# A scan's unused operand read from a PSUM bank, and new instruction lengths in the order planner

## The chip, the cores and the metric

The kernel runs on one core of one Trainium2 chip. The metric is the device time of one execution in microseconds (us); three executions of the kernel before took 1605.84, 1606.33 and 1608.09 us, median 1606.33 us. A profiled execution of it spans 1604.8 us from its first to its last instruction.

## What is computed

One layer of a hybrid block on 2048 tokens of width 1024, in fp32:

```python
hn = rmsnorm(h, mix_norm_g)
u, g_ssm, q, k, v, g_attn = split(hn @ w_in)                 # six times 512 columns
y_ssm = glu(gelu(s5_scan(u))) * silu(g_ssm)                  # diagonal complex SSM, 32 groups
y_att = stick_breaking(rmsnorm(q), rmsnorm(k), v) * silu(g_attn)   # 8 heads of 64
h = h + concat(y_ssm, y_att) @ w_out
h = h + sigmoid(rmsnorm(h) @ w_pg) * (p @ w_pp)
```

The change sits in the attention. For a block of 128 queries, with `z = q k^T / 8`:

```python
log_stay = where(s < t, log_sigmoid(-z), 0)
later    = reverse_cumsum(log_stay) - log_stay               # over the keys after s
weights  = where(s < t, exp(log_sigmoid(z) + later), 0)
out      = weights @ v
```

The kernel computes the same with products: `sigmoid(-z)` is multiplied up from the last key to the first, and each `sigmoid(z)` is multiplied with the running product of the keys behind it.

## The kernel before

**Stages.** The program falls into three stretches of the span. Up to about 345 us it normalizes and turns x, projects u (`phase_u`), prepares and runs the S5 scan (`ssm_chain`, `ssm_pack`, `ssm_batch`) and the SSM gate (`gate_unit`). From 345 us to about 1180 us it runs the attention, four pairs of heads (`hp`) whose 16 query blocks are swept with a skew of 8 steps, mixed with the projections of the blocks to come (`attn_proj`, matmuls L657 to L659 into `ps_qk`) and, in its last quarter, with the GLU (`glu_unit`, matmuls L542 to L544 into `ps_g` and `ps_v`). From there to the end it runs the output projection and the per-layer embedding (`out_block`, `ple_block`), which are TensorE work almost alone.

**One attention step** (`attn_block`) handles one chunk of up to 512 keys for two heads `h`. On TensorE (PE) six matmuls, L718, fill two PSUM tiles `z`, one for each head. For each head ScalarE (ACT) writes `px = sigmoid(-z)`, L723, and `be = sigmoid(z)`, L728. On the chunk of the diagonal GpSimd (POOL) masks both, L732. VectorE (DVE) runs the product through `px` in place, from the last key to the first, L734; its first element is the one the next chunk goes on from (`carry`, copied by L727). POOL multiplies `be` with the shifted `px`, L736. PE turns `be` into two PSUM tiles `ps_wt`, 16 transposes for a full chunk, L527 in `transposes`; ACT (L745) or DVE (L743) copies them to `ws`; PE multiplies with v into `ps_o`, L753. So what follows a chunk's `z` goes round PE, ACT, (POOL,) DVE, POOL, PE, ACT, PE.

**The scan.** L734 is a `tensor_tensor_scan` with `op0=mult` and `op1=bypass`: the state is multiplied with the first operand, and the second is read but not used. Before the change both operands are `px`, which lies in SBUF.

**PSUM.** There are eight banks with names. The `z` tiles go round three of them, "z0", "z1" and "tr", and round "z0" and "z1" alone in the last eight of the 40 steps (`BANKS`, `glu_at`). A bank is written again when all readers of its last tile are done.

**The order** of all instructions on every engine, and of the DMAs on their queues, is made before the run by a planner. `plan` collects each instruction's dependences from the memory it touches, and a length from `duration`: a pair of the time that the engine is taken and of a delay until the result can be used. `list_schedule` then goes through the program as if it ran, always giving the engine that is free first the instruction with the lowest rank that is ready; on PE a change between full matmuls, matmuls over 64 rows and matmuls over 64 columns costs `change=0.2`, and work of the present kind is preferred by `near=4.0`. `best_order` repeats this forwards and backwards six times and keeps the shortest plan; `arrange` fixes that order on each engine. Reads of a PSUM tile count as writes in `plan`, so a bank's readers stand one behind the other in the order of the program. The lengths are thus not times of the run, but they decide what stands where in all five queues.

Of the kernel before, what the change touches and what calls it, by code (L numbers as in the profile page):

```python
# [13 lines left out]
ALU = mybir.AluOpType  # L14
# [686 lines left out]
def attn_block(e, pool, A, i):  # L701
# [3 lines left out]
    nc = e.nc  # L705
    q, g = A.q.pop(i)
    half = [slice(HD * h, HD * (h + 1)) for h in range(HPP)]
    carry = [None] * HPP
    po = e.bank("ps_o", *e.o_banks)
    held = []  # L710
    for ch in range(i // 4, -1, -1):
        nb = min(4, i + 1 - 4 * ch)
        n = nb * P
# [6 lines left out]
        for h, z in enumerate(zs):  # L720
            be = e.buf("be", [P, 512], BEB, BEX)
            px = e.buf("px", [P, 513], PXB, PXX)
            nc.scalar.activation(px[:, :n], z[:, :n], AF.Sigmoid, scale=-(HD ** -0.5))  # L723
            if carry[h] is None:
                nc.gpsimd.memset(px[:, n:n + 1], 1.0)
            else:
                nc.vector.tensor_copy(px[:, n:n + 1], carry[h])  # L727
            nc.scalar.activation(be[:, :n], z[:, :n], AF.Sigmoid, scale=HD ** -0.5)  # L728
            if ch == i // 4:
                for a, fill in ((px, 1.0), (be, 0.0)):  # L730
                    d = a[:, n - P:n]
                    nc.gpsimd.affine_select(d, d, pattern=[[-1, P]], compare_op=ALU.is_gt, fill=fill, base=0, channel_multiplier=1)  # L732
            rv = px[:, :n][:, ::-1]
            nc.vector.tensor_tensor_scan(rv, rv, rv, initial=1.0 if carry[h] is None else carry[h], op0=ALU.mult, op1=ALU.bypass)  # L734
            carry[h] = px[:, 0:1]
            nc.gpsimd.tensor_tensor(be[:, :n], be[:, :n], px[:, 1:n + 1], op=ALU.mult)  # L736
            bes.append(be)
        w = e.buf("ws", [P, HPP, 4, P], WSB, WSX)
# [310 lines left out]
def duration(i, name, outs, ins, psum):  # L1049

    n = max([a[1] for a in outs + ins] or [1])
    eng = str(i.engine).split(".")[-1]
    if name == "InstDMACopy":
        return (0.6 if eng == "Pool" else 0.45), 0.0
    if name == "InstMatmult":
        cols, kind = outs[0][1], ins[0][2]
        if i.is_transpose:
            return (0.031 if ins[0][0] <= 64 else 0.109), 0.12
        if "float32r" in kind or "bfloat16" in kind:
            return {512: 0.228, 256: 0.120}.get(cols, max(cols / 2255.0, 0.058)) / (2 if ins[0][0] <= 64 else 1), 0.12  # L1060
        half = min(outs[0][0], ins[0][0]) <= 64
        return (1 if half else 2) * max(cols / 1160.0, 0.056), 0.12
    if eng == "Activation":
        return 0.193 + n * 0.00082, 0.0
    if eng == "Pool":
        if name == "InstTensorTensor" and "pow" in str(i.op).lower():
            return 0.45 + 0.15 * n, 0.0
        base, slope = {"InstMemset": (0.1, 0.0008), "InstTensorCopy": (0.5, 0.001), "InstTensorScalarPtr": (0.3, 0.001), "InstTensorScalarAffineSelect": (0.35, 0.0008)}.get(name, (0.47, 0.00175))
        return base + slope * n, 0.0
    if name == "InstTensorScalarPtr" and i.is_tensor_tensor_scan:  # L1070
        return 0.22 + n * 0.0027, 0.0
    if name in ("InstMemset", "InstTensorCopy") and not psum:
        return 0.11 + n * 0.0006, 0.0
    return 0.15 + n * 0.00107, 0.0


def plan(tc, pools):
# [3 lines left out]
    open_l, open_r, base, slots, spans, over, home, used = [], [], {}, {}, [], {}, {}, {}  # L1081
# [23 lines left out]
    for k, i in enumerate(mybir_i):  # L1105
        if type(i).__name__ == "BassTilePoolBoundary":
            pre.append(set())
            soft.append({number[q] for q in over.get(i.name, [])} | used.get(i.name, set()))
            length.append((0.0, 0.0, 0))
            continue  # L1110
        need, ins, outs, loose, psum = set(), [], [], set(), False
        for w, accs in ((0, i.ins), (1, i.outs)):
            for a in accs:
                b = getattr(a, "bass_ap", None)
# [4 lines left out]
                for s, c in a.ap[1:]:  # L1119
                    n *= int(c)  # L1120
                (outs if w else ins).append((int(a.ap[0][1]), n, str(a.dtype)))
                if type(t).__name__ != "Tile":
                    continue
                shape = tuple(int(x) for x in t.shape)
# [44 lines left out]
        loose.discard(k)  # L1169
        pre.append(need)  # L1170
        soft.append(loose - need)
        length.append(duration(i, type(i).__name__, outs, ins, psum) + ((outs[0][0] * outs[0][1] * 4 if type(i).__name__ == "InstDMACopy" else 0),))
        if type(i).__name__ == "InstMatmult":
            mode[k] = "rows" if ins[0][0] <= 64 else "cols" if outs[0][0] <= 64 else "all"
    return mybir_i, pre, soft, length, mode


_seen = {}
# [9 lines left out]
def list_schedule(ops, pre, soft, length, mode, rank, near=4.0, change=0.2):  # L1188
# [4 lines left out]
    after, open_, free, wait, ready, order, now = [[] for _ in ops], [len(p) + len(q) for p, q in zip(pre, soft)], {}, {}, {}, {}, {}  # L1193
    start, done, link = [0.0] * n, [0.0] * n, 0.0
    for k in range(n):
        for q in (*pre[k], *soft[k]):
# [16 lines left out]
    for _ in range(n):  # L1213
# [115 lines left out]
```

## Time and profile before

| what | value |
|---|---|
| median of three runs | 1606.33 us |
| span of the profiled execution | 1604.8 us |
| first `ps_z` matmul of the attention | 345.0 us |
| last `ps_z` matmul | 1171.2 us |
| DVE busy, 350 to 1200 us | 682.6 of 850 us |
| POOL busy, 350 to 1200 us | 634.6 of 850 us |
| ACT busy, 350 to 1200 us | 561.1 of 850 us |

The profile lists, for groups of instructions, a busy time and a mean duration; for stretches of the span, the busy time of each engine and the clock that TensorE was granted (1.00 is full); and a chain of waits, which goes back from the last instruction, at each step to what released it. Matmuls are pipelined, so the duration of one in the groups is longer than the time from one to the next; the pieces of the chain give that time.

### The profile page before, as it was taken

The numbers are of one execution on the slowest core, as the hardware profiler recorded it, in microseconds if no ns is written. First come the engines' busy times: TensorE is split into PE (matmuls) and PEld (weight loads), VectorE is DVE, ScalarE is ACT, GpSimd is POOL, SyncE is SP. The second block draws the span as 40 slices with busy tenths as digits, with TensorE's granted clock in tenths as the row PEclk, the third lists the DMA queues.
The fourth block names the chain that finished last, engine by engine and source line by source line (L and its number), as shares of the span: only waits on it lengthen the run. The fifth ranks groups of instructions, "written<-read, shape, count | busy, mean of one in ns | idle before, by whom it ended". The sixth has DMA issues, their size and how long they took to land.

```text
span 1604.8 us, 31108 instructions
## 1 busy us (share of the span) xinstructions
PE 1548.5 (96%) x11878; PEld 1254.5 (78%) x11878; DVE 1079.1 (67%) x1980; ACT 825.2 (51%) x1850; POOL 766.3 (48%) x882
## 2 busy tenths in 40 slices
PE   6999898999999999999999999999989999999998
PEld 6998888987777777777777776777678788888887
DVE  6895948868678997789987899748764432332322
ACT  6643435456566776677766777646544221121211
POOL 2242434437578898688967798747630000000000
PEclk9999999999999999999999999999999999999999
DMA  9897535455332323323233234432354221212210
GB/s 294 262 289 194 175 118 181 156 174 193 113 113 84 112 91 132 113 85 108 95 132 112 86 109 112 109 96 68 107 164 126 83 79 50 86 60 69 64 49 33
DMA packets 147670, 195.58 MB, mean 122 GB/s; under 512 B 63697, under 2 KB 110753, under 8 KB 136129
## 3 DMA queue, kind: packets, MB, share of 16 engines
q1 hardware_dynamic: 145552, 186.45, 36.1%
q0 software_dynamic: 1968, 7.15, 2.2%
q8 instruction: 94, 1.54, 0.4%
q14 instruction: 56, 0.45, 0.1%
HBM read 145.44 MB, written 48.12 MB: 121 GB/s over the span
## 4 chain that ended last, share of the span: by engine, by line
PE 79%; DVE 11%; issue 4%; POOL 3%; ACT 1%; DMA 1%; SPq 0%; POOLq 0%; DVEq 0%; ACTq 0%
PE ps_qk L657 7%; PE ps_qk L659 7%; PE ps_qk L658 7%; PE ps_o L753 6%; PE ps_z L718 5%; PE ps_wt L527 4%; PE ps_g L659 4%; PE ps_h L657 4%; PE ps_h L658 4%; PE ps_g L658 4%; PE ps_h L659 4%; PE ps_g L657 4%; DVE px L734 3%; POOL be L736 2%; PE ps_u L543 2%
## 5 line engine op out<-in xcount | busy, mean ns | idle before, releaser
L736 POOL TENSOR_TENSOR be<-be,px 128x512 f32<-128x512 f32 (+3 forms) x320 | 404.1, 1275 | 136.6 <-DVE px L734 51.0
L734 DVE TENSOR_TENSOR_SCAN px<-px 128x512 f32<-128x512 f32 (+3 forms) x320 | 424.6, 1338 | 52.6 <-ACT px L723 37.0
L723 ACT ACTIVATE px<-ps_z 128x512 f32<-128x512 f32 (+3 forms) x320 | 170.0, 539 | 78.8 <-PE ps_z L718 51.9
L657 PE MATMUL ps_qk<-w_w,xt 128*128 128x512 f32 x480 | 198.7, 414 | 1.2 <-DVE gn L60 1.2
L658 PE MATMUL ps_qk<-w_w,xt 128*128 128x512 f32 x480 | 195.4, 407 | 0.0
L659 PE MATMUL ps_qk<-w_w,xt 128*128 128x512 f32 x480 | 195.3, 407 | 0.0
L508 POOL TENSOR_TENSOR rs_h<-rs_h,mhalf 128x1 f32<-128x1 f32 x16 | 9.1, 572 | 381.8 <-DVE rs_h L67 381.8
L728 ACT ACTIVATE be<-ps_z 128x512 f32<-128x512 f32 (+3 forms) x320 | 170.4, 545 | 5.4 <-PE ps_wt L527 5.4
L745 ACT ACTIVATE ws<-ps_wt 128x512 f32<-128x512 f32 (+3 forms) x256 | 129.0, 540 | 79.3 <-PE ps_wt L527 78.5
L718 PE MATMUL ps_z<-k,q 64*128 64x512 f32 (+3 forms) x960 | 138.5, 392 | 2.4 <-ACT be L728 1.5
L753 PE MATMUL ps_o<-ws,v 128*64 128x128 f32 x2176 | 138.3, 278 | 0.0
L753 PEld LDWEIGHTS ps_o<-ws,v 128*64 128x64 f32 x2176 | 118.7, 138 | 22.2 <-issue 18.1
L527 PEld LDWEIGHTS ps_wt<-ident,be 64*128 64x128 f32 x2176 | 83.1, 138 | 51.6 <-issue 25.6
L657 PEld LDWEIGHTS ps_qk<-w_w,xt 128*128 128x128 f32 x480 | 90.2, 188 | 32.1 <-issue 11.9
L659 PEld LDWEIGHTS ps_qk<-w_w,xt 128*128 128x128 f32 x480 | 90.3, 188 | 24.2 <-issue 5.7
L658 PEld LDWEIGHTS ps_qk<-w_w,xt 128*128 128x128 f32 x480 | 90.5, 189 | 23.5 <-issue 5.8
L527 PE MATMUL ps_wt<-ident,be 64*128 64x64 f32 x2176 | 102.9, 229 | 5.8 <-POOL be L736 2.8
L514 ACT ACTIVATE yr<-yt 128x512 fp32r<-128x512 f32 x32 | 20.2, 632 | 162.7 <-PE ps_h L659 157.3
L657 PE MATMUL ps_h<-w_w,yr 128*128 128x512 f32 x256 | 100.7, 393 | 2.3 <-ACT yr L514 2.3
L659 PE MATMUL ps_g<-w_wg,hr 128*128 128x512 f32 x256 | 101.5, 397 | 0.0
L658 PE MATMUL ps_g<-w_wg,hr 128*128 128x512 f32 x256 | 101.1, 395 | 0.0
L658 PE MATMUL ps_h<-w_w,yr 128*128 128x512 f32 x256 | 100.6, 393 | 0.0
(378 smaller groups left out, 3608.5 us busy)
## 6 DMA issues: line engine op xcount, KB each, us to landing
xt<-hn SPq DMA_DIRECT2D x60, 1024.0 KB, 4.9
hn<-xt SPq DMA_DIRECT2D x16, 1024.0 KB, 9.5
wst<-in_w_in_dram SPq DMA_DIRECT2D x48, 256.0 KB, 5.3
xg<-hn SPq DMA_DIRECT2D x12, 1024.0 KB, 7.0
x<-in_x_dram SPq DMA_DIRECT2D x16, 512.0 KB, 7.0
out_dram<-o SPq DMA_DIRECT2D x32, 256.0 KB, 2.0
h<-in_x_dram SPq DMA_DIRECT2D x15, 512.0 KB, 4.3
u<-uq POOLq DMA_DIRECT2D x4, 1024.0 KB, 18.3
```

The source lines that it names most:

```text
L527: e.nc.tensor.transpose(ps[h][:, 64 * k:64 * k + 64], v[r], e.ident[r, r])
L543: mm(out, wh, xl, start=False, stop=False)
L657: mm(out, xh, wh, start=first, stop=False)
L658: mm(out, xh, wl, start=False, stop=False)
L659: mm(out, xl, wh, start=False, stop=last)
L718: nc.tensor.matmul(z[:, :n], q[half[h], a], A.k[ch][half[h], b, :n], start=s == 0, stop=s == 2)
L723: nc.scalar.activation(px[:, :n], z[:, :n], AF.Sigmoid, scale=-(HD ** -0.5))
L728: nc.scalar.activation(be[:, :n], z[:, :n], AF.Sigmoid, scale=HD ** -0.5)
L734: nc.vector.tensor_tensor_scan(rv, rv, rv, initial=1.0 if carry[h] is None else carry[h], op0=ALU.mult, op1=ALU.bypass)
L736: nc.gpsimd.tensor_tensor(be[:, :n], be[:, :n], px[:, 1:n + 1], op=ALU.mult)
L745: nc.scalar.activation(dst, ps, AF.Copy)
L753: nc.tensor.matmul(po[half[h], :P], A.v[sb][:, h], w[:, h, b], start=sb == i, stop=sb == 0)
```

## The change

The scan reads `z`, where it lies in PSUM, as its second operand. As before, the operand's values are not used. The planner gets other lengths for most instructions, and a resource that it did not have: an instruction that `shares` marks (a GpSimd instruction that reads SBUF, a DVE instruction with two operands in SBUF, or a DVE copy or scalar instruction from SBUF to SBUF) does not start before the last one so marked has ended.

```diff
-            nc.vector.tensor_tensor_scan(rv, rv, rv, initial=1.0 if carry[h] is None else carry[h], op0=ALU.mult, op1=ALU.bypass)
+            nc.vector.tensor_tensor_scan(rv, rv, z[:, :n][:, ::-1], initial=1.0 if carry[h] is None else carry[h], op0=ALU.mult, op1=ALU.bypass)
...
         if i.is_transpose:
-            return (0.031 if ins[0][0] <= 64 else 0.109), 0.12
+            return (0.031 if ins[0][0] <= 64 else 0.109), 0.11
         if "float32r" in kind or "bfloat16" in kind:
-            return {512: 0.228, 256: 0.120}.get(cols, max(cols / 2255.0, 0.058)) / (2 if ins[0][0] <= 64 else 1), 0.12
+            return max(cols / 2400.0 + 0.0136, 0.107) / (2 if ins[0][0] <= 64 else 1), 0.11
...
     if eng == "Activation":
-        return 0.193 + n * 0.00082, 0.0
+        return (0.05 if psum else 0.094) + n * 0.00083, 0.065 if psum else 0.03
     if eng == "Pool":
         if name == "InstTensorTensor" and "pow" in str(i.op).lower():
-            return 0.45 + 0.15 * n, 0.0
-        base, slope = {"InstMemset": (0.1, 0.0008), "InstTensorCopy": (0.5, 0.001), "InstTensorScalarPtr": (0.3, 0.001), "InstTensorScalarAffineSelect": (0.35, 0.0008)}.get(name, (0.47, 0.00175))
-        return base + slope * n, 0.0
+            return 0.35 + 0.15 * n, 0.08
+        base, slope = {"InstMemset": (0.04, 0.0008), "InstTensorCopy": (0.4, 0.001), "InstTensorScalarPtr": (0.25, 0.001), "InstTensorScalarAffineSelect": (0.14, 0.0008)}.get(name, (0.12, 0.00186))
+        return base + slope * n, 0.09
     if name == "InstTensorScalarPtr" and i.is_tensor_tensor_scan:
-        return 0.22 + n * 0.0027, 0.0
-    if name in ("InstMemset", "InstTensorCopy") and not psum:
-        return 0.11 + n * 0.0006, 0.0
-    return 0.15 + n * 0.00107, 0.0
+        return 0.05 + n * 0.0022, 0.03
+    if name in ("InstMemset", "InstTensorCopy", "InstTensorScalarPtr") and not psum and not i_tt(i):
+        return 0.07 + n * 0.0006, 0.03
+    return 0.07 + n * 0.00104, 0.03
...
+def shares(i, name, read, psum):
+
+    eng = str(i.engine).split(".")[-1]
+    if eng == "Pool":
+        return read > 0 and name != "InstDMACopy"
+    return eng == "DVE" and (read > 1 or (read == 1 and not psum and name in ("InstTensorCopy", "InstTensorScalarPtr")))
...
+        if length[k][3]:
+            t = max(t, port)
+            port = t + length[k][0]
```

No instruction is added or removed; all five queues are put in another order. On PE the attention gets other neighbours around the `z` tiles. The rows of PE around the pair of tiles `ps_z_6375` and `ps_z_6376` (one chunk of one query block, two heads; `ps_qk` is a projection, `ps_o` the product with v), before:

```order
L718 MATMUL ps_z_6375<-k_5136,q_5966 128x512
L718 MATMUL ps_z_6376<-k_5136,q_5966 128x512 [waits Activation_49]
L718 MATMUL ps_z_6375<-k_5136,q_5966 128x512
L718 MATMUL ps_z_6376<-k_5136,q_5966 128x512
L718 MATMUL ps_z_6375<-k_5136,q_5966 128x512
L718 MATMUL ps_z_6376<-k_5136,q_5966 128x512
L657 MATMUL ps_qk_6302<-w_w_4966,xt_6300 128x512
L658 MATMUL ps_qk_6302<-w_w_4966,xt_6300 128x512
```

and with the change:

```order
L718 MATMUL ps_z_6375<-k_5136,q_5966 128x512
L718 MATMUL ps_z_6376<-k_5136,q_5966 128x512 [waits DVE_49]
L718 MATMUL ps_z_6375<-k_5136,q_5966 128x512
L718 MATMUL ps_z_6376<-k_5136,q_5966 128x512
L718 MATMUL ps_z_6375<-k_5136,q_5966 128x512
L718 MATMUL ps_z_6376<-k_5136,q_5966 128x512
L753 MATMUL ps_o_6030<-ws_6061,v_5642 64x128 x2
L753 MATMUL ps_o_6030<-ws_6061,v_5344 64x128 x2
```

The bank is now waited for on DVE (its last reader is the scan) where it was on ACT, and behind the tiles stands other work.

On ACT the two sigmoids of the two heads `ps_z_10187` and `ps_z_10188` (another chunk) stood apart, before:

```order
L723 ACTIVATE px_10196<-ps_z_10187 128x512 [waits DVE_49,Pool_49]
L728 ACTIVATE be_10195<-ps_z_10187 128x512
L492 ACTIVATE w_w_10500<-wst_10501,gmix_121 128x512 [waits DMAHW2_49]
L694 ACTIVATE k_9268<-ps_tq_10025,gqk_2008 128x128 [waits DVE_49]
L723 ACTIVATE px_10203<-ps_z_10188 128x512 [waits Activation_49,Pool_49]
L514 ACTIVATE q_10077<-ps_tq_10078 128x128 [waits PE_49]
L728 ACTIVATE be_10202<-ps_z_10188 128x512
```

and stand together with the change:

```order
L723 ACTIVATE px_10196<-ps_z_10187 128x512 [waits PE_49,Activation_49,Pool_49]
L723 ACTIVATE px_10203<-ps_z_10188 128x512 [waits PE_49,DVE_49,Activation_49,Pool_49]
L728 ACTIVATE be_10195<-ps_z_10187 128x512
L697 ACTIVATE g_10086<-ps_tq_10078 128x128 [waits DVE_49]
L728 ACTIVATE be_10202<-ps_z_10188 128x512
```

On DVE the scans of the same two heads (the listing calls the scan SCALAR_TENSOR_TENSOR; `px_10196` and `px_10203`) had four instructions between them, before:

```order
L734 SCALAR_TENSOR_TENSOR px_10196<-px_10196,px_10141 128x512 [waits Activation_49]
L71 SCALAR_TENSOR_TENSOR k_9268<-ps_tq_10025,gqk_2008,k_9268 128x128 [waits Activation_49]
L60 TENSOR_TENSOR q_10077<-ps_tq_10078,q_10077 128x128 [waits Activation_49]
L60 TENSOR_TENSOR yat_9979<-ps_o_9886,g_9332 128x128 [waits DMAHW2_49]
L727 COPY px_10203<-px_10148 128x1 [waits DVE_49,Pool_49]
L734 SCALAR_TENSOR_TENSOR px_10203<-px_10203,px_10148 128x512
```

and follow each other with the change, each with its `z` tile as an operand:

```order
L727 COPY px_10196<-px_10141 128x1 [waits DVE_49]
L727 COPY px_10203<-px_10148 128x1 [waits DVE_49,Pool_49]
L71 SCALAR_TENSOR_TENSOR w_w_10515<-wst_10516,gmix_121,w_w_10515 128x512 [waits DMAHW7_49,Activation_49]
L734 SCALAR_TENSOR_TENSOR px_10196<-px_10196,px_10141,ps_z_10187 128x512 [waits Activation_49]
L734 SCALAR_TENSOR_TENSOR px_10203<-px_10203,px_10148,ps_z_10188 128x512 [waits Activation_49]
```

The two copies that start the scans moved ahead of both, and the small instructions between the scans elsewhere.

More of the change, by code (lines that the diff above doesn't have):

```diff
@@ L1121, in plan @@
                 (outs if w else ins).append((int(a.ap[0][1]), n, str(a.dtype)))
+                read += not w and n > 1 and type(t).__name__ == "Tile" and slots_space(slots, t.tag) == "SB"
                 if type(t).__name__ != "Tile":
```

12 lines of the change are left out of this document (8 added, 4 removed).

## The prediction

> **What bounds the kernel now.** I read the busy table first, then the stretches of the span, then the chain of waits, and last the groups that the change touches.
>
> ```profile
> PE 1548.5 (96%) x11878; PEld 1254.5 (78%) x11878; DVE 1079.1 (67%) x1980; ACT 825.2 (51%) x1850; POOL 766.3 (48%) x882
> PE 79%; DVE 11%; issue 4%; POOL 3%; ACT 1%; DMA 1%; SPq 0%; POOLq 0%; DVEq 0%; ACTq 0%
> 0.00:50.00 50.00, 34.22 (x318) 32.24 (x319) 34.96 (x140) 31.42 (x52) 15.53 (x26) 0.99 0.82 265
> 50.00:350.00 300.00, 281.14 (x2256) 271.80 (x2255) 225.44 (x479) 144.33 (x313) 107.06 (x71) 0.95 0.64 195
> 350.00:950.00 600.00, 597.42 (x5435) 445.94 (x5436) 495.14 (x885) 413.49 (x1034) 470.92 (x611) 1.00 0.33 113
> 950.00:1200.00 250.00, 237.43 (x1924) 181.21 (x1921) 187.43 (x261) 147.59 (x297) 163.66 (x160) 0.97 0.39 109
> 1200.00:1604.00 404.00, 398.26 (x1954) 323.25 (x1952) 136.11 (x219) 88.33 (x156) 9.14 (x16) 1.00 0.23 71
> ```
>
> The first row is the share of each engine; PE is busy for 96% of the span. The second is the chain of waits by engine: 79% of it is PE. The others are stretches; after each length stand the busy time of PE, weight loads, DVE, ACT and POOL, then PE's granted clock. PE lacks 15.8 us at the start (the first data), 18.9 us from 50 to 350, 2.6 us in the first 600 us of attention, 12.6 us in its last part, 5.7 us in the output stage. The last is not touched: no scan runs there, and POOL is busy 9 us of 404. So the attention, where the change works, can give back 15.2 us of idle PE, and 0.03 x 250 = 7.5 us where the clock was 0.97: **22.7 us, or 1.4%, is all that a perfect DVE and POOL could bring there**. The chain shows where it was lost, in stretches such as
>
> ```profile
> 976.11 1.14 POOL be L736
> 977.24 0.80 issue
> 978.04 1.20 POOL be L736
> ...
> 1091.60 1.19 DVE px L734
> ...
> 1174.81 6.51 DMA yt<-ys
> 1181.34 0.64 ACT yr L514
> ```
>
> (start, length, what): scans and multiplications end last there, 0.8 us lies between two multiplications, and the attention's last piece waits for a load that no scan is part of.
>
> **The scan's operand.** The groups, by form:
>
> ```profile
> L734 DVE TENSOR_TENSOR_SCAN px<-px 128x512 f32<-128x512 f32 x224 | 343.3, 1542 | 44.2 <-ACT px L723 37.0 <-POOL px L732 7.0
> L736 POOL TENSOR_TENSOR be<-be,px 128x512 f32<-128x512 f32 x224 | 322.1, 1450 | 117.0 <-DVE px L734 36.2 <-ACT be L728 29.4 <-DVE px L727 22.7
> L728 ACT ACTIVATE be<-ps_z 128x512 f32<-128x512 f32 x224 | 133.5, 610 | 4.2 <-PE ps_wt L527 4.2
> L723 ACT ACTIVATE px<-ps_z 128x512 f32<-128x512 f32 x224 | 133.2, 603 | 68.2 <-PE ps_z L718 46.2 <-POOL be L736 5.2 <-POOL glus L648 3.4
> L450 DVE TENSOR_TENSOR_SCAN rot<-decf,rot 128x512 f32<-128x512 f32 x8 | 9.8, 1225 | 0.3
> L60 DVE TENSOR_TENSOR o<-o,h 128x512 f32<-128x512 f32 x32 | 22.1, 691 | 1.0
> L60 DVE TENSOR_TENSOR h<-ps_h,h 128x512 f32<-128x512 f32 x32 | 22.0, 691 | 98.2 <-PE ps_h L659 98.2
> ```
>
> A scan over 512 takes 1542 ns on average in the attention, where POOL is busy three quarters of the time, and 1225 ns (L450, also two SBUF operands) before it. POOL's product takes 1450 ns on average and 1.1 to 1.2 us in the chain's pieces. So the two slow each other down, by 0.32 and 0.30 us each time. With one operand in PSUM I take the scan at 1225 ns. The trace has no scan from PSUM; the bounds are 1225 (nothing lost by PSUM, as h<-ps_h with one PSUM operand and o<-o,h with none both take 691) and 1542 (the two still collide). I take the lower, since it is the same operation at the same width. That frees 224 x 0.317 = 71 us of DVE and, at 1.15 us, 224 x 0.30 = 67 us of POOL. Both lie beside PE, so their price on the path is not 138 us but a share of the 22.7 us. Four of these belong to the load at 1174.81 and the slow matmuls after it, and some of the rest was other DVE work. I take half: **-11 us** (ends 0 and -19).
>
> [...]
>
> **The wait that it adds.** A reader of a bank waits for the reader ahead of it:
>
> ```profile
> DVE v L674 <- ACT qn L673: 25.0, 15, 3.4
> PE ps_z L718 <- ACT be L728: 1.5, 3, 0.6
> ```
>
> (who waited for whom, in total, times, longest): `v` and `qn` are copied from different columns of one bank, and DVE waits for ACT. So the scan will wait for the second sigmoid, 0.61 us later than now, and the next `ps_z` on the bank for the scan instead of that sigmoid, which today costs PE 1.5 us in all. Behind a late `ps_z` stands all of PE's queue; in the first order shown above that is `ps_o` now. From the end of `ps_z` to a second head's finished `be` the floor is, with the change, four sigmoids at some 0.5 to 0.6 us from one to the next (2.2), a scan (1.2), a product (1.15) and handoffs (0.4): 5.0 us. Before it was two sigmoids and the first head's scan (0.6 + 1.5), a scan (1.5), a product (1.45), handoffs (0.3): 5.4 us.
>
> What covers this is the PE work that stands between a head's `ps_z` and its first transpose. Its lengths are read from pieces of the chain:
>
> ```profile
> 783.42 0.64 PE ps_wt L527 x16
> 784.06 0.43 PE ps_qk L658
> 784.49 0.23 PE ps_qk L659
> 784.72 0.23 PE ps_qk L657
> 784.95 0.90 PE ps_z L718 x6
> ...
> 787.38 1.90 PE ps_o L753 x32
> ```
>
> A matmul over 512 takes 0.23 us, and 0.43 after work of another kind, so a change of kind costs 0.20; a chunk's transposes 0.64, its `ps_z` 0.90, two chunks of `ps_o` 1.90, each with its change. Counted through both PE orders at these lengths, a full-width head has a median of 10.7 us of such work before and 8.1 with the change; under 7 us have 13 of 224 heads before and 58 with the change, under 6 us 4 and 9. For full-width tiles the PE work until the bank is written again has a median of 6.1 us before and 6.4 with the change, and is nowhere under 2.8 then, where a sigmoid pair and a scan need 1.1 + 1.2 = 2.3. So the floor is covered nearly everywhere, but with 3 us to spare where there were 5. I take five more heads that wait 0.4 us: **+2 us** (ends 0 and +22, see the first rival).
>
> **The order.** The new lengths change no instruction. They take ACT, DVE and POOL as shorter, and so place a chunk's steps closer. On PE there are 556 changes of kind where there were 539, 17 x 0.20 = **+3.4 us**. Before 350 us PE lacks 18.9 us and ran at 0.95, 0.05 x 281 = 14 us; what ended its longest idle times there is
>
> ```profile
> PE ps_x L527 <- ACT x L561: 13.0, 2, 11.2
> PE ps_qk L657 <- DVE b_en L60: 4.9, 1, 4.9
> PE ps_b L407 <- ACT stB L359: 4.6, 1, 4.6
> PE ps_b L407 <- DMA us<-u: 3.5, 1, 3.5
> ```
>
> The first belongs to the start, the others are three single places where PE ran out of filling work. A new order will have some of these and others; a planner that knows the collisions should have fewer. I take one of the three away: **-4 us** (ends -12 and +10, the three gone, or two more). The start stays: DVE's first scale factor now stands behind a copy that waits for a small load, but POOL, which needs it next, was taken by DMA issues until 9.3 us anyway:
>
> ```profile
> 8.64 0.64 POOL L215 DMA_DIRECT2D dsk<-in_ssm_d_dram  x1 [0.29 <-POOL dsk L197]
> 9.35 0.57 POOL L508 TENSOR_TENSOR rs_x<-rs_x,mhalf 128x1 f32<-128x1 f32 x1
> ```
>
> **Sum.** -11 + 2 + 3.4 - 4 = -9.6 us on the span of 1604.8, so 1595. The median of the runs lies 1.5 us over that span: **1597 us**.
>
> **Rivals.** *First: the cover is too thin (slower).* If a head needs 7 us in the run, not 5, PE waits where the cover is less. For the 58 - 13 = 45 heads, some 22 pairs, at 0.7 us each, that is 15 us, with +3.4 for the changes of kind, nothing gained, and the span's 1.5: 1626. For it: DVE and POOL stay busy for some 0.7 and 0.65 of the attention, so a scan often stands behind something; PE has waited almost nowhere because the cover was generous. Against it: both queues lose a tenth of their load. It decides from about 6.5 us between `ps_z` and `be`.
> *Second: nothing changes.* PE had 2.6 us to win in 600; if the last part's idle time is from the GLU's splits on DVE and not from the scans, the gain is 3 us and the changes of kind eat it: 1606.
> *Third: the early stage falls worse.* Two more idle times of 5 us, the rest as forecast: -11 + 2 + 3.4 + 10 = +4.4, 1611.
> *Fourth: the change does not do what it says.* Scan and product still slow each other; then the plan is made for 1.2 us scans and gets 1.5, 0.6 us more for a pair and 5.6 us from `ps_z` to `be`: about half the first rival's waits, 8 us, +3.4: 1618.
> *Fifth: more than forecast.* The whole -19, all three early idle times (-12), +3.4: 1578.
>
> **How the numbers follow.** Forecast 0.39, first rival 0.22, second 0.12, third 0.10, fourth 0.05, fifth 0.12. A change of 0.2%, 3.2 us, is what a measurement of this kernel can tell. Of the forecast's own range, 1588 to 1604, nearly all is faster; with the fifth and a little of the second and third: faster 0.51, same 0.13, slower 0.36. The range that holds 8 in 10 must reach to the fifth and to most of the first: 1576 to 1626.
>
> **What would show it.** Right: scans near 1.23 us and POOL's products near 1.15 in the groups, DVE under 610 us and POOL under 570 between 350 and 1200 us, PE idle there under 10 us. The first rival: `ps_z` waits for L734, or the transposes for L736, for more than 10 us in total. The fourth: scans still at 1.5. The third: the first `ps_z` of the attention later than now. The forecast is wrong as soon as PE's idle time in the attention grows, whatever DVE gains.

## The result, and the profile after

The changed kernel takes 1608.12 us (median of 12 runs, 1604.82 to 1613.18); the one before, run beside it, 1607.49 us (12 runs). The ratio is 1.001, with an interval of 1.000 to 1.002: **no change that can be told**, where 1597 us were forecast. The profiled execution has a span of 1606.2 us, 1.4 us more than the one before.

Of the page's busy times after, and of the same five stretches as in the prediction (length, then busy PE, weight loads, DVE, ACT, POOL, PE's granted clock):

```profile
PE 1553.5 (97%) x11878; PEld 1256.4 (78%) x11878; DVE 969.8 (60%) x1980; ACT 820.2 (51%) x1850; POOL 599.4 (37%) x882
```

```profile
0.00:50.00 50.00, 33.02 (x295) 30.60 (x295) 40.21 (x225) 29.45 (x50) 16.30 (x26) 0.99 0.76 255
50.00:350.00 300.00, 279.96 (x2293) 268.86 (x2294) 201.07 (x402) 149.05 (x326) 105.17 (x84) 0.96 0.66 202
350.00:950.00 600.00, 595.67 (x5310) 444.50 (x5309) 424.78 (x867) 399.79 (x1006) 342.80 (x587) 0.99 0.33 110
950.00:1200.00 250.00, 245.43 (x2030) 188.16 (x2031) 167.78 (x271) 153.64 (x316) 126.92 (x172) 0.99 0.39 109
1200.00:1604.00 404.00, 399.45 (x1954) 324.31 (x1952) 136.00 (x219) 88.23 (x155) 8.25 (x15) 1.00 0.23 71
```

DVE lost 109 us and POOL 167 us of work, and PE's end hardly moved. The groups of after, by form, show that the operand did what it should:

```profile
L734 DVE TENSOR_TENSOR_SCAN px<-px,ps_z 128x512 f32<-128x512 f32 x224 | 275.3, 1260 | 96.7 <-ACT be L728 84.6 <-POOL px L732 11.2
L736 POOL TENSOR_TENSOR be<-be,px 128x512 f32<-128x512 f32 x224 | 252.9, 1129 | 266.3 <-DVE px L734 233.0 <-DVE px L727 9.6 <-PE ps_qk L659 6.9
```

The scan went from 1542 to 1260 ns and POOL's product from 1450 to 1129: they no longer slow each other down. The means hide two groups of instructions: before, 107 of the 224 full-width scans took under 1.3 us (1.27 on the average), and the longest took 2.48; after, all 224 take under 1.3 us (1.26). Of the full-width products 123 took under 1.15 us before (1.09 on the average), and the longest took 2.12; after, 200 take under 1.15. So before, a scan or a product ran at its own length or was held up, by up to 1.2 and 1.0 us; the 0.32 and 0.30 us that the prediction had for "each time" are averages over both groups.

The idle columns have turned over as well. Before, the scan waited 37 us for the first sigmoid (L723) and the product 36 us for the scan; now the scan waits 85 us for the second sigmoid (L728), which reads the same bank ahead of it, and the product 233 us for the scan. The chain of a head has become a row of steps that wait for one another, on engines with room to spare.

To see where PE's time went I counted PE's matmuls in the timelines, weighed each with its time to the next one (0.23 us for 512 columns, and so on; 1416 us in all), and read off when each kernel had done the same work. The difference, after minus before (negative where after is ahead), is +6.4 us at 87 us of the span before (the `ps_u` stage), -12.7 at 311 us, +1.1 at 391 us, +9.9 at 941 us and +1.3 at 1385 us. So the S5 stage gave 19 us and 14 of them were lost where the attention begins; the attention itself lost 9 and won them back. They were won back in its last part: between 950 and 1200 us PE's idle time fell from 12.6 to 4.6 us and the clock rose from 0.97 to 0.99. Where the 9 us went is not shown: between 350 and 950 us the idle time grew only from 2.6 to 4.3 us. The two places of loss ahead of the attention:

**The hand-over to the attention.** PE's timeline after (start, length, what; in brackets the idle time ahead of it and what ended it):

```profile
332.85 0.28 PE L544 MATMUL ps_sg<-xg,w_w 128*128 128x256 f32 x1
334.06 0.72 PE L718 MATMUL ps_z<-k,q 64*128 64x128 f32 x7 [0.93 <-DVE sg L60]
337.30 1.01 PE L718 MATMUL ps_z<-k,q 64*128 64x256 f32 x5 [2.53 <-DVE px L734]
341.08 0.37 PE L527 MATMUL ps_wt<-ident,be 64*128 64x64 f32 x2 [2.77 <-POOL be L736]
342.34 0.37 PE L527 MATMUL ps_wt<-ident,be 64*128 64x64 f32 x2 [0.89 <-POOL be L736]
...
345.51 0.69 PE L753 MATMUL ps_o<-ws,v 128*64 128x128 f32 x4 [1.59 <-ACT ws L745]
...
349.03 0.79 PE L657 MATMUL ps_qk<-w_w,xt 128*128 128x512 f32 x1
349.62 0.63 PE L658 MATMUL ps_qk<-w_w,xt 128*128 128x512 f32 x1
...
353.42 0.39 PE L659 MATMUL ps_qk<-w_w,xt 128*128 128x512 f32 x1
353.65 0.40 PE L657 MATMUL ps_qk<-w_w,xt 128*128 128x512 f32 x1
```

of its stretches there (columns as above)

```profile
334.00:349.00 15.00, 7.06 (x40) 4.33 (x40) 8.19 (x14) 7.83 (x23) 7.66 (x24) 0.56 0.72 241
349.00:352.60 3.60, 3.60 (x9) 2.81 (x9) 2.16 (x2) 3.06 (x6) 2.27 (x7) 0.50 0.00 0
352.60:358.00 5.40, 5.40 (x24) 4.40 (x23) 3.09 (x6) 0.98 (x3) 1.79 (x2) 0.98 0.06 9
```

with the first of them before,

```profile
334.00:349.00 15.00, 13.17 (x109) 12.12 (x108) 7.42 (x13) 7.70 (x20) 3.09 (x11) 1.00 0.61 213
```

and, of ACT's timeline after, at the same place, one row:

```profile
340.44 0.28 ACT L723 ACTIVATE px<-ps_z 128x128 f32<-128x128 f32 x1 [3.91 <-DMA z<-gsq]
```

The S5 stage's matmuls end at 333 us, 11 us sooner than before, but `ps_qk`, the work that stood on PE beside the first heads, starts only 349 us into the span, 1 us later than before (348.1). Until then the first, narrow heads are alone on PE, and each step of their chain is waited for: 8.7 us in the five brackets, where before had three, of 0.93, 0.42 and 0.48 us. The second head's `px` waits 3.9 us for the last store of the S5 stage (`z<-gsq`, issued at 336.9), which reads what lies in its buffer.

And PE's clock is low. From 334 to 349 us PE is busy 7.1 us and was granted 0.56; before, it was busy 13.2 us in the same stretch and was granted 1.00. Until 352.6 us the clock stays at 0.50, and matmuls of 512 columns, which follow each other every 0.23 us afterwards, take 0.43. By an estimate from these rows that is worth 0.44 x 7.06 + 0.50 x 3.60 = 4.9 us. For the work between the two marks PE is idle 2.3 us before (311 to 391 us) and 10.4 us after (298.3 to 392.1 us): 8.2 us more, which with the clock makes 13.1 of the 13.8 us between -12.7 and +1.1.

**The `ps_u` stage.** Who waited there for whom between 17 and 140 us, before and after:

```profile
ACT x L561 <- POOL rs_x L508: 2.4, 5, 0.9
```

```profile
ACT x L561 <- POOL rs_x L508: 16.3, 9, 4.1
```

The new order puts the S5 stage's preparation earlier on DVE and POOL (in the stretch from 0 to 50 us DVE is busy 40.2 us where it was 35.0), and ACT gets the scale factor of x, a power that POOL computes behind DVE, later. The last `ps_u` matmul starts at 133.6 us and not at 126.5.

### The profile page after: what moved, and what is told of

Read it like the earlier page. It is cut to its first block, busy times and chain, and to the rows that moved or that the text cites. A ratio compares the mean times of both kernels' runs of the same rounds, so it can differ in the third digit from the quotient of the medians.

```text
span 1606.2 us, 31293 instructions
## 1 busy us (share of the span) xinstructions
PE 1553.5 (97%) x11878; PEld 1256.4 (78%) x11878; DVE 969.8 (60%) x1980; ACT 820.2 (51%) x1850; POOL 599.4 (37%) x882
## 5 line engine op out<-in xcount | busy, mean ns | idle before, releaser
L736 POOL TENSOR_TENSOR be<-be,px 128x512 f32<-128x512 f32 (+3 forms) x320 | 317.2, 996 | 275.9 <-DVE px L734 242.0
L734 DVE TENSOR_TENSOR_SCAN px<-px,ps_z 128x512 f32<-128x512 f32 (+3 forms) x320 | 337.5, 1084 | 122.3 <-ACT be L728 87.3
L723 ACT ACTIVATE px<-ps_z 128x512 f32<-128x512 f32 (+3 forms) x320 | 158.8, 537 | 96.1 <-PE ps_z L718 69.6
L728 ACT ACTIVATE be<-ps_z 128x512 f32<-128x512 f32 (+3 forms) x320 | 163.1, 555 | 0.0
L718 PE MATMUL ps_z<-k,q 64*128 64x512 f32 (+3 forms) x960 | 145.8, 397 | 3.9 <-DVE px L734 2.7
L718 PEld LDWEIGHTS ps_z<-k,q 64*128 64x128 f32 x960 | 80.9, 188 | 42.2 <-issue 25.2
L657 PE MATMUL ps_h<-w_w,yr 128*128 128x512 f32 x256 | 100.3, 392 | 0.2 <-DVE h L60 0.2
```

Of the source, the lines that this page charges most:

```text
L657: mm(out, xh, wh, start=first, stop=False)
L718: nc.tensor.matmul(z[:, :n], q[half[h], a], A.k[ch][half[h], b, :n], start=s == 0, stop=s == 2)
L734: nc.vector.tensor_tensor_scan(rv, rv, z[:, :n][:, ::-1], initial=1.0 if carry[h] is None else carry[h], op0=ALU.mult, op1=ALU.bypass)
```

## The experiments

Two questions: what the operand is worth by itself, and what the order is worth by itself. "Relief" is what it gives that scan and product no longer slow each other. For the first, orders were written in. "Written in" means that `arrange` takes each engine's sequence from a table:

```diff
 def arrange(tc, pools, rows):
-    ops, pre, *rest = plan(tc, pools)
-    _, order, _ = best_order(ops, pre, *rest, rows)
+    ops = plan(tc, pools)[0]
...
```

The table at the end of this section has all of them.

**1. Before's order, operand from z (e4).** A z step whose bank isn't free is put behind the next step that can go.

> The kernel of before in its own fixed order (the planner switched off, the order of before written in), and only the scan's second operand read from z; a z step whose bank the scan still holds is put behind the next step that can go (106 of 10502 rows on PE). Theory: the operand by itself is a gain, and the new order gives it back. The idle time of PE between 350 and 1200 us was 15.15 us before; with the full-width scan near 1.26 us in place of 1.54 and the POOL product near 1.13 in place of 1.45, some 6 to 10 us of that and of the lowered clock go: 1597 to 1602. Rival one: holding z's bank until the scan has ended costs what the shorter scan gains: waits of ps_z for L734 over 6 us, time 1605 to 1610. Rival two: VectorE and GpSimd were never what PE waited for, so that their relief is worth nothing: L734 and L736 shorter, no waits for L734, 1606 to 1609.

Measured: 1717.34 us, ratio 1.069 (1.067 to 1.071). Neither the theory nor a rival had that; the first rival's waits came, 58.9 us of them where it said over 6. Of this kernel's waits, PE's and DVE's:

```profile
PE ps_z L718 <- DVE px L734: 58.9, 55, 2.6
```

```profile
DVE px L734 <- ACT be L728: 147.9, 95, 6.9
```

Its groups show scan and product as fast as in after (1265 and 1119 ns). But before's order put the second sigmoid where nobody hurried for it; now the scan stands behind it, up to 6.9 us, everything on DVE behind the scan, and PE behind the bank. From 350 to 1200 us PE is idle 64.9 us where it was 15.2, at a clock of 0.97. In an order that doesn't know of it the new wait costs 111 us, what the operand gives already taken off.

**2. After's order, operand from px (e3).**

> The changed kernel in its own fixed order (the order of after written in, the planner switched off), and only the scan's second operand put back to px. Theory: the operand is a gain at any fixed order, so that it is slower than after by 6 to 10 us: 1612 to 1618, with L734 512 wide back near 1.54 us and L736 near 1.45. Rival one (the bank hold costs what the shorter scan gains): 1605 to 1609, the ps_z waits for L734 gone. Rival two (VectorE and GpSimd are never waited for): 1606 to 1609.

Measured: 1623.62 us, ratio to before 1.0106 (1.0092 to 1.0121), so 15.5 us slower than after. One row each of its windows and of PE's waits:

```profile
350.00:1200.00 850.00, 826.99 (x7247) 617.77 (x7247) 641.21 (x1125) 546.83 (x1311) 609.23 (x762) 0.99 0.33 106
```

```profile
PE ps_wt L527 <- POOL be L736: 12.4, 11, 3.9
```

The scan is back at 1406 ns only, the product at 1459. PE is idle 23.0 us there, and in after 8.9:

```profile
350.00:1200.00 850.00, 841.10 (x7339) 632.66 (x7338) 592.56 (x1137) 553.43 (x1321) 469.71 (x758) 0.99 0.35 110
```

At an order that was made for it the operand is a gain, as the theory said, and a larger one than the 6 to 10 us it named. Both rivals fall.

**3 and 4. One part alone, planned anew:** the operand from z with the planner of before (e1), the scan on px with the planner of after (e2). The diff is that of the change, of which the first has the line L734 and the second all the others.

> The operand read from z, with the planner of before (old lengths, no shared resource), which plans anew around the longer hold of z's bank. Theory (operand a gain, new order of the new planner a loss): 1596 to 1603. Rival one (the bank hold takes the gain): 1605 to 1612. Rival three: any re-planning scatters the time by as much as the whole gain, so that neither part has a cost of its own: anywhere in 1596 to 1616, and its stages before the attention differ from both kernels'.

> The new planner (lengths and the shared resource of VectorE and GpSimd), with the scan's second operand left on px. Theory (the new planner's order costs about what the operand gains): 1612 to 1620, with the stall at the hand-over to the attention and in the ps_u stage as in after. Rival one (the bank hold is the loss, the planner is neutral): 1603 to 1609. Rival three (scatter of re-planning): anywhere in 1596 to 1616.

Measured: 1613.70 us, ratio 1.0046 (1.0032 to 1.0060), and 1619.77 us, ratio 1.0085 (1.0072 to 1.0098). The second lies in its theory's range, the first in none but that for scatter, 1596 to 1616, which left it open whether its 7.7 us mean anything. In these two draws each part alone is a loss, and together they are none: neither cost is a term that can be added.

**5. What relief could be worth at before's order (e5).** The product is cut to one column, which leaves out part of the attention's weights; the order is written in:

```diff
-            nc.gpsimd.tensor_tensor(be[:, :n], be[:, :n], px[:, 1:n + 1], op=ALU.mult)
+            nc.gpsimd.tensor_tensor(be[:, :1], be[:, :1], px[:, 1:2], op=ALU.mult)
```

> The kernel of before in its own fixed order, with GpSimd's product be*px (L736) cut to one column, so that part of the attention's weights is left out and VectorE's scans have nothing of it beside them: it shows the most that relief from contention can be worth where the bank of z is held no longer. Theory now (PE in before's order was covered against slow scans and products, so that little of its waiting hung on them): the scans fall to 1.25 to 1.35 us, the PE time from the first to the last ps_z (825.6 us in before) falls by no more than 7, and the time is 1599 to 1605. Rival (the relief is worth the 11 us and more that the prediction took, and after's order spoils it): 1588 to 1596.

Measured: 1586.83 us, ratio 0.9883 (0.9869 to 0.9896): 20 us, beyond what either side had expected.

```profile
350.00:1200.00 850.00, 846.76 (x7463) 638.66 (x7462) 588.78 (x1163) 567.13 (x1348) 324.31 (x765) 1.00 0.36 115
```

PE's idle time falls to 3.2 us and the clock is 1.00. This takes away the product's own place in the chain too, so it is a bound. It stays inside the prediction's bound of 22.7 us, and my new theory that PE had been covered falls.

**6. A second operand that is neither px nor z (e6):** at before's order, a column of a constant in SBUF, repeated along the row.

```diff
-            nc.vector.tensor_tensor_scan(rv, rv, rv, initial=...
+            nc.vector.tensor_tensor_scan(rv, rv, e.mhalf[:, :1].to_broadcast([P, n]), initial=...
```

> The kernel of before in its own fixed order; the scan's unused second operand is one column of a constant in SBUF, repeated along the row, so that neither px is read a second time nor z's bank held longer. If the second read of SBUF is what VectorE and GpSimd contend for, whatever its addresses, L734 512 wide stays at 1.5 us and the time at 1604 to 1608. If a repeated column isn't read from SBUF each time, L734 falls to 1.25 to 1.3 us and L736 to 1.15, and the time goes where the run with the cut product goes: 1599 to 1605 by the theory that PE was covered, 1588 to 1596 by its rival.

Measured: 1607.47 us, ratio 1.0002 (0.9993 to 1.0011), by the first theory. Its groups:

```profile
L734 DVE TENSOR_TENSOR_SCAN px<-px,mhalf 128x512 f32<-128x512 f32 x224 | 340.9, 1531 | 44.2 <-ACT px L723 37.3 <-POOL px L732 6.7
L736 POOL TENSOR_TENSOR be<-be,px 128x512 f32<-128x512 f32 x224 | 320.1, 1441 | 117.4 <-DVE px L734 32.7 <-ACT be L728 30.7 <-DVE px L727 24.0
```

It is the second operand in SBUF that collides, a constant's column as much as `px` (1531 ns against 1542 for the scan, 1441 against 1450 for the product). Relief without the bank's hold isn't to be had this way.

**7 to 12. How far re-planning alone scatters (e9 to e14).** One constant of the planner is changed by less than 1%, in before and in after:

```diff
-        return 0.22 + n * 0.0027, 0.0
+        return 0.22 + n * 0.00271, 0.0
```

> Before, with the planner's slope of the scan raised from 0.0027 to 0.00271 (the planned scan of 512 columns goes from 1.602 to 1.608 us), which describes nothing better or worse but lets the planner order the work anew. Theory with scatter (any re-planning moves the time by several us): outside 1604 to 1608, between 1598 and 1620. Theory without (the time follows the lengths' fitness): 1604 to 1608.

> After, with the planner's slope of the scan raised from 0.0022 to 0.00221 (the planned scan of 512 columns goes from 1.176 to 1.182 us). Theory with scatter: outside 1605 to 1610, between 1596 and 1622. Theory without: 1605 to 1610.

> Before, with the planner's slope of the scan at 0.00269 in place of 0.0027. Theory (the order that a planner with nearly the same lengths happens to find is worth up to 16 us either way, so that before and after are two draws from two overlapping heaps): between 1588 and 1616, more than 3 us from 1606, the changes of kind on PE (533 against 539) no guide to it. Rival (before is the ordinary result and the run at 1591 an odd one): 1603 to 1609.

> Before, with the planner's slope of the scan at 0.00272. Theory: between 1588 and 1616, more than 3 us from 1606. Rival: 1603 to 1609.

> After, with the planner's slope of the scan at 0.00219 in place of 0.0022. Theory of the two heaps: between 1588 and 1618, more than 3 us from 1608. If the operand's gain (15.5 us at after's own order) holds on the average over orders, the three neighbours of after lie lower than the three of before by some 8 to 15 us; if what it costs in freedom of the order (z's bank held until the scan has ended, 111 us lost at before's order) takes the gain, the two means lie within 6 us.

> After, with the planner's slope of the scan at 0.00222. Theory: between 1588 and 1618, more than 3 us from 1608; with the neighbours of both sides, as for the run before.

Measured: 1591.20 us, 1606.53 and 1591.86 for the neighbours of before; 1595.50, 1599.11 and 1605.13 for those of after. The theory with scatter was right in kind, not in its ranges: 1591.20 and 1595.50 lie below them (from 1598 and from 1596), and 1606.53 and 1605.13 are within 3 us of the kernel whose neighbours they are, where more was expected. A constant that differs by 6 ns in a scan can move the time by 15 us. The four of each kind average 0.995 and 0.997 of before: 3 us apart, less than their spreads of 16 and 13 us. The neighbours alone average 0.9936 and 0.9958, within the 6 us that were named for a gain taken back. Of the windows, one of before's kind and one of after's:

```profile
350.00:1200.00 850.00, 834.90 (x7408) 636.40 (x7407) 674.85 (x1150) 565.50 (x1335) 612.28 (x757) 0.99 0.35 112
```

```profile
350.00:1200.00 850.00, 844.40 (x7407) 637.15 (x7406) 596.60 (x1151) 559.45 (x1333) 469.07 (x759) 1.00 0.36 112
```

What doesn't scatter: PE's idle time in this stretch is 14.4 to 15.2 us in the four of before's kind and 5.6 to 8.9 in the four of after's. That is the relief, 7 us on the average (the lengths changed with the operand). Nor does what stands against it: 499 to 539 changes of kind on PE in the one, 546 to 562 in the other, 30.75 more on the average, times 0.20 us is 6.2 us. And every kernel with the new lengths in its early stage has lost 5 to 10 us at 87 us of before's span, in `ps_u`, and none with the old ones has.

**13. The early steps with the old lengths (e15)** (what stands in front of the attention's first `ps_z` in the program; the attention keeps the new ones).

```diff
+        early = k < 3470
-        length.append(duration(i, ...
+        length.append((duration_early if early else duration)(i, ... not early and shares(...
```

> After, but the planner uses before's lengths, and no shared resource, for every step in front of the attention's first ps_z in the program; the attention on keeps the new ones. Theory (the new lengths cost 7 to 10 us in the ps_u stage, which the hand-over hands on): the last ps_u matmul back from 133.6 to about 126, the last store z<-gsq issued before 335, and the time 1590 to 1601. Rival (the early stage's loss is caught up anyway, because the hand-over waits for something else): the last ps_u at 126, the time 1603 to 1610.

Measured: 1600.09 us, ratio 0.9961 (0.9948 to 0.9973). The stores of the S5 stage, of this kernel and of after (the times are first and last start):

```profile
L476 SPq DMA_DIRECT2D z<-gsq x16: 319/320/418, 175.3 to 329.4; - x16
```

```profile
L476 SPq DMA_DIRECT2D z<-gsq x16: 319/320/979, 181.7 to 336.9; - x16
```

The last `ps_u` starts at 126.4 us, the last store is issued 7.5 us sooner, and a lead of 9 us is left after the hand-over. Stage and time came as the theory said, though a time alone, within the 13 us that this kind scatters over, would prove little. By the count of PE's work this kernel leads by some 14 us at 311 us of before, hardly more than after's 12.7: the loss in `ps_u` had been made up by then, and what differs is the hand-over, which takes 5 us here and 14 in after. In the table, the kernels that keep 9 us or more are the three whose last store is issued by 332 us, whatever their operand.

**14. Fewer changes of kind (e16):** after, with `near=6.0` for `near=4.0` in `list_schedule`.

> After, with the planner's bias against a change of kind on PE (near) raised from 4 to 6 us: 530 changes in the program's order in place of 556. Theory (each change costs its 0.20 us, and nothing else is lost): 5 us less, 1600 to 1605, with the early stage as in after. Rival (fewer changes mean later z steps and more waiting): the idle time of PE between 350 and 1200 us over 12 us in place of 8.9, and 1606 to 1615. The scatter of re-planning (both kinds spread over 13 to 16 us so far) can cover either, so that the split into busy and idle time counts more than the sum.

Measured: 1606.80 us, ratio 1.0005 (0.9996 to 1.0014), within the rival's range.

```profile
350.00:1200.00 850.00, 837.10 (x7316) 634.55 (x7315) 584.13 (x1133) 547.17 (x1315) 464.60 (x754) 0.99 0.34 109
```

26 changes fewer, 5.2 us at 0.20 each, and 4.0 us more idle time (12.9): in this order the one was bought with the other, and in the attention ("added" in the table) 2.0 us were lost.

**15 and 16. A second draw of the two mixed kernels (e17, e18),** with the slopes 0.00271 and 0.00221.

> The operand alone with the old planner (as e1_operand_only), its slope of the scan at 0.00271. The order holds some 50 to 60 changes of kind more than before's (588 in e1). Theory (the old lengths with z's bank held are a bad match: too many changes of kind): 1607 to 1618. Rival (e1 was a bad draw): 1592 to 1603.

> The new planner alone, scan on px (as e2_planner_only), its slope of the scan at 0.00221. Theory (lengths that are too short for scans and products that do contend give an order with too little cover, so that PE waits some 20 us in the attention): 1612 to 1622, idle time of PE between 350 and 1200 us over 18 us. Rival (e2 was a bad draw): 1595 to 1608.

Measured: 1614.71 us, ratio 1.0052 (1.0036 to 1.0069), and 1634.12 us, ratio 1.0174 (1.0158 to 1.0190). The first lies in its theory's range; the second is 12 us beyond its own, with the idle time that the theory named. Its windows:

```profile
350.00:1200.00 850.00, 826.24 (x7152) 617.82 (x7151) 644.88 (x1116) 539.62 (x1297) 581.91 (x748) 0.98 0.32 103
```

PE is idle 23.8 us; its scans and products take 1549 and 1400 ns in an order planned for 1.18 and 1.07 us. The other has 599 changes of kind: the old lengths with the bank's hold.

**17. The early stage of e9 joined to the attention of e10 (e19),** written in.

> Scan's operand from z; the order is written in: every step in front of the attention's first ps_z in the program as in e9_before_jitter, every later one as in e10_after_jitter, shifted so that the first ps_z comes where it did in the former. Theory (the two parts add: 9.5 us gained by the hand-over there, 10.5 us in the attention here): 1583 to 1591, the last store z<-gsq by 333 us. Rival (the attention's gain came of what its own early stage had left ready, so that the joint is worse than either): 1592 to 1606.

Measured: 1628.15 us, ratio 1.0139 (1.0125 to 1.0153), worse than either expectation. Of PE's waits:

```profile
PE ps_qk L657 <- DVE gsq L60: 21.0, 1, 21.0
PE ps_y L467 <- ACT tp L461: 15.8, 3, 14.4
```

Both lie in the S5 stage, where the first pair's projections and the loads for the second are interleaved with it; joining two orders put steps there ahead of what they need. From the hand-over on it won 10.0 us against before, as its model did (10.5): the attention's part carries over, the early part doesn't survive the cut.

**18. The operand at another fixed order (e20):** that of e10, with the operand from px.

> The order of e10_after_jitter (1595.5 us with the scan's operand from z), written in, with the operand put back to px. Theory (relief from contention is a gain at a fixed order that was made for z): 10 to 25 us slower, 1606 to 1620, L734 512 wide over 1.4 us, the idle time of PE between 350 and 1200 us up from 5.6 to 13 to 25. Rival (the 15.5 us were peculiar to after's order): 1593 to 1602.

Measured: 1620.57 us, ratio 1.0091 (1.0076 to 1.0105): 25 us slower than with z, at the upper end of what the theory named; the scan takes 1466 ns.

```profile
350.00:1200.00 850.00, 827.14 (x7289) 618.80 (x7288) 649.41 (x1127) 547.97 (x1312) 590.00 (x757) 1.00 0.34 107
```

Idle time 22.9 us for 5.6.

All runs, grouped by operand and by the lengths that made the attention's order. Lead: the difference to before's profile in us at equal PE work, at 391 us of before (negative is ahead), and what is added from there to the end. Idle: PE from 350 to 1200 us. Changes: of kind, in PE's order. Store: the start of the last `z<-gsq`.

| kernel | operand, lengths | ratio | lead at 391 | added | idle | changes | store |
|---|---|---|---|---|---|---|---|
| before | px, old | 1 | 0 | 0 | 15.2 | 539 | 341.2 |
| e9 | px, old | 0.9907 | -9.5 | -7.3 | 15.1 | 499 | 331.9 |
| e11 | px, old | 1.0001 | +0.5 | -0.6 | 14.9 | 536 | 338.3 |
| e12 | px, old | 0.9900 | -10.2 | -3.8 | 14.4 | 517 | 329.3 |
| after | z, new | 1.0010 | +1.1 | 0.0 | 8.9 | 556 | 336.9 |
| e10 | z, new | 0.9934 | -1.6 | -10.5 | 5.6 | 546 | 339.7 |
| e13 | z, new | 0.9952 | -4.9 | -3.2 | 8.6 | 550 | 332.8 |
| e14 | z, new | 0.9989 | -1.3 | 0.0 | 7.8 | 562 | 336.9 |
| e15, old lengths early | z, new | 0.9961 | -9.0 | +1.7 | 9.4 | 555 | 329.4 |
| e16, near 6 | z, new | 1.0005 | -2.0 | +2.0 | 12.9 | 530 | 334.7 |
| e1 | z, old | 1.0046 | -2.5 | +11.4 | 19.4 | 588 | 336.4 |
| e17 | z, old | 1.0052 | -0.5 | +9.5 | 14.2 | 599 | 340.3 |
| e2 | px, new | 1.0085 | -1.2 | +14.4 | 20.2 | 511 | 337.7 |
| e18 | px, new | 1.0174 | -1.7 | +28.5 | 23.8 | 531 | 339.0 |
| e3 | px, after's order | 1.0106 | +2.7 | +14.7 | 23.0 | 556 | 338.9 |
| e20 | px, e10's order | 1.0091 | -1.3 | +13.4 | 22.9 | 546 | 338.8 |
| e4 | z, before's order | 1.0688 | +14.1 | +99.6 | 64.9 | 543 | 343.0 |
| e5, product cut | px, before's order | 0.9883 | -0.8 | -19.2 | 3.2 | 539 | 340.1 |
| e6, constant | before's order | 1.0002 | +0.5 | +1.3 | 15.1 | 539 | 341.8 |
| e19 | z, joined | 1.0139 | +31.4 | -10.0 | 15.1 | 547 | 365.4 |

## Why the prediction was wrong

**The scan's operand, -11: the mechanism right, the term of the wrong kind.** Scan 1260 ns (1225 taken), product 1129 (1150), DVE 592.6 us and POOL 469.7 from 350 to 1200 us (under 610 and 570 said), PE's idle time there 8.9 (under 10 said). So every sign that was named for being right came, and the time did not: the signs watched the attention's engines and not what its order would cost. The bound of 22.7 us held: 20 with the product cut. What failed is the working that took half of that bound and added it to the price of a new order (half of what it had left after taking off four is 9.4, not 11). In after 6.3 us of idle time were won (15.2 to 8.9), and from 391 us on the time moved by 0.0. The relief is 15.5 and 25 us at an order that suits it, and -111 at the one that stood there; which order is made is the other part of the change. In the four orders of after's kind 7 us of idle time were won.

**The scan's length from z.** A full-width scan from z takes 1260 ns (after) to 1265 (e4); the 107 on px that took under 1.3 us before average 1267. Their time, rather than the 1225 of L450, was the price to take.

**The wait that it adds, +2.** The scan waits for the second sigmoid as described (85 us in all), and nowhere full-width did `ps_z` wait long: 2.5 of its 2.7 us lie at the hand-over. But the cover was counted on full-width heads alone. The narrow heads at the attention's start, which have next to none of it, were left out, and the idle time after is there.

**The order, +3.4 for the changes of kind.** The count held for after (556) and for its kind: 30.75 more on the average over four, 6.2 us at the price read from the chain. The price itself, 0.20 us, rests on single pieces of the chain; no run tests it alone. With the 7 us of the relief it leaves 0.9, and the attention's added lead is -3.4 us on the average in after's kind and -2.9 in before's.

**The order, -4 for the early stage, and "the start stays": the other step that failed.** In its own place the term came out better than taken. Of the three waits named, two are all but gone (4.9 and 4.6 us, of which 0.3 is left; the third is 4.4 for 3.5), and at 311 us of before the changed kernel leads by 12.7 us, although the start did not stay: 6.4 us were lost in `ps_u`, for the preparation that the new lengths put ahead of the scale factors. What failed is that time won ahead of the attention was taken to last. The hand-over took 13.8 us: measured +1.1 where -4 was taken. The prediction looked at three waits of PE, and not at what the attention's first steps need: filling work beside them on PE, and the last store of the stage ahead. The sign named for the third rival, a later first `ps_z`, would have misled too: it came 11 us earlier (334.1 for 345.0). That the store's time decides is argued, not shown: it is read from one wait and from the order of the rows in the table, among them the run that changed the early lengths alone; the buffer that both share was not moved. A wait of `px` for that store, of 2.0 to 3.9 us, stands in e2, e3, e13, e14 and e16 too; but e10 and e11 have none and lose some 9 and 6 us at the hand-over all the same, so it is not the whole cause.

**The sum.** By these steps -9.6 was forecast: -4 to the hand-over and -5.6 after it. Measured +1.1 and 0.0: the two steps missed by 5.1 and 5.6 us. Of the second only a part is traced, as where the attention lost its 9 us stays open. Two of the rivals' sums are off by 1 us (their terms give 1625 and 1579). Of the rivals the second had the number (1606), and not the reason: there was something to win. The first's mechanism showed, in a place where it wasn't looked for, and at 8 us.

**What no step spoke of:** that the planner's order is itself a draw. A neighbour of before with the same instructions is at 0.990, one of after at 0.993. A term of 4 or 11 us can't be carried over from the profile of one draw to another. What stays open is why z's hold comes with more changes of kind: the runs show that it does, with old lengths (588 and 599) more than with new ones.

The fastest run of a complete kernel is a neighbour of before at 1591.2 us (0.9907), with the operand on px; of those with z it is 1595.5 us. Both beat the two kernels compared. The best of a dozen draws, they are no evidence for one operand over the other.

## What to carry to other kernels

Where a planner decides the order, test a change at a fixed order, and the order by itself: here the same operand was worth -111, +15.5 and +25 us, and with the new lengths, over four orders of each kind, nothing that a scatter of 13 to 16 us lets one tell. Before a re-planned kernel is compared, change a constant that means nothing, a few times, and see how far the time moves; only what all draws of one kind share (idle time of one stretch, changes of kind, a late stage) is the change's own. And a stage that ends sooner gave nothing here where the next one's filling work and the last store ahead of it did not come sooner too.

## What the hardware showed that was not expected

POOL's masks on a 128 x 128 block, one operand in SBUF, were slowed as well. Before, then after:

```profile
L732 POOL TENSOR_SCALAR_AFFINE_SELECT be<-be 128x128 f32<-128x128 f32 x128 | 85.3, 668 | 3.3 <-ACT be L728 3.1
```

```profile
L732 POOL TENSOR_SCALAR_AFFINE_SELECT be<-be 128x128 f32<-128x128 f32 x128 | 39.0, 312 | 9.0 <-ACT be L728 8.0 <-DVE px L734 0.2
```

So scans on px more than doubled the time of a mask on the average: 43 of the 128 took under 0.33 us before (0.29 on the average), 121 after, and the longest before took 1.32 us, 1.0 us more than those 43. At after's own order with px (e3) the mean is 627 ns for 312. And a repeated column of a constant collides like a full operand (1531 ns against 1542): the second operand needs no memory of its own size to count.
